# 192 bytes of padding in front of the norm's output: one SBUF offset for both operands of the large products

## The chip, the cores and the metric

The kernel runs on one core of one Trainium2 chip, as one launch. Times are device microseconds; the kernel before takes 1121.89 us (median of 3 runs, 1121.78 to 1123.58). TensorE (PE) multiplies: an instruction LDWEIGHTS puts a 128 x 128 operand into the array (the stationary operand, `lhsT`), and MATMUL streams the other one (the moving operand, `rhs`) past it into a bank of PSUM. VectorE (DVE) and ScalarE (ACT) work on the tiles in SBUF, and SyncE (SP) issues nearly all DMAs. SBUF has 128 partitions; a tile's address is its byte offset in each partition. This text calls the address modulo 2048 the residue of a tile.

## The reference, cut to what matters

One decoder layer with 512 tokens and a width of 1024, in float32:

```python
h = _rms(x, norm1_w) * (1 + sc1) + sh1               # sc1, sh1, g1, ... = silu(c) @ w_ada + b_ada
z, xbc, dt, q, k, v, u, gates = split(h @ w_in)      # 11,280 columns
x = x + g1 * ((g_ssd*y_ssd + g_attn*y_attn + g_pool*y_pool) @ w_out)
h = _rms(x, norm2_w) * (1 + sc2) + sh2
x = x + g2 * (square(relu(h @ w_ff1)) @ w_ff2)       # 4096 wide between the two
```

`y_ssd`, `y_attn` and `y_pool` are a Mamba-2 scan, a dilated window attention and a pooling over windows, each followed by a projection to 1024 columns. Most of the arithmetic is the large products with `w_in`, `w_ssd_out`, `w_attn_out`, `w_pool_out`, `w_out`, `w_ff1` and `w_ff2`.

## The kernel before, in words

Each large product is done three times over, in float32r: both operands are split into a high part and a low part, and `mm3` (lines 284 to 287) sums low x high, high x high and high x low in one PSUM bank. Three MATMULs of 512 columns, one from each of the lines 285, 286 and 287, make a triple; a 512-column strip of a weight with 1024 rows is 8 x 4 = 32 triples.

Weights come from DRAM two row blocks at a time into `raw` (pool `raws`, three buffers), ACT writes their high part `wh`, and DVE their low part `wl` (pool `wsp`, three buffers each, line 267). `wstream` (line 274) does this ahead of the products by a scheduling priority.

Two forms of product exist. In `gemm_feat` (line 289) the weight tile is stationary, 128 of its columns at a time, and the activation streams. In `gemm_tok` (line 301) it is the other way round: 128 tokens of the activation are stationary and the weight streams. There the 128 tokens either lie one after the other or, for two of the three attention groups (`mod=True`), are every fourth token, so that the stationary operand is read with a step of four elements (`toks`, line 298).

Where the tiles lie, in the order in which the pools are opened (lines 102 to 106) and filled. `cpool` begins at 16512 with `cst` (constants, 328 columns, 1312 bytes) and then holds the 16 tiles of the norm's output, 2048 bytes each: `hh`, `hl` (high and low part after the first norm), whose places `gh`, `gl` take over after the second norm. `sm` has small tiles (`vec`, `ones`, statistics), among them no operand of a large product. Then follow `raws`, `wsp` and `gp`; the latter has the 59 blocks of 2048 bytes from which `blk` takes every other activation (`a` after the squared ReLU, `yn`, `pool`, `o`, `mx`) and the resident weights (`wsh`, `wsl` at the start, `wrh`, `wrl` near the second norm).

What reads the norm's output, by the names of the trace (a row says `psacc<-moving,stationary`, and an ending h or l is the high or low part):

- streaming, from `hh`, `hl` and `gh`, `gl`: rows `psacc<-hl,wh` and its like, 416 triples (13 strips), and `psacc<-gl,wh`, 224 triples (7 strips);
- stationary, tokens one after the other: `psacc<-wsl,hh`, 64 triples (the first query and key strips, lines 456 to 482, in an order written out by hand), and 32 of the 224 triples `psacc<-wl,hh` (the first value strip);
- stationary, every fourth token: the other 192 triples `psacc<-wl,hh`, 6 strips;
- streaming 256 columns at a time past resident weights (`ff_rows`, line 1129): `psacc<-gl,wrh`, 64 triples.

Of the kernel before, what the change touches and what calls it, by code (L numbers as in the profile page):

```python
# [10 lines left out]
F32 = mybir.dt.float32  # L11
# [6 lines left out]
P = 128  # L18
# [80 lines left out]
def kernel(ctx: ExitStack, tc: tile.TileContext, a: dict, out: bass.AP, dbg=None):  # L99
    nc = tc.nc  # L100

    cpool = ctx.enter_context(tc.tile_pool(name="cpool", bufs=1))
# [9 lines left out]
    def uid(s):  # L112
        cnt[0] += 1
        return f"{s}_{cnt[0]}"

    class Slots:
# [12 lines left out]
        def free(self, t):  # L129
            self.idle.append(self.used.pop(id(t))[0])  # L130
# [3 lines left out]
    def blk(name, dt=F32):  # L134
        return sb.take(name, dt)
# [5 lines left out]
    def small(shape, name, bufs=1, dt=F32):  # L141
        return sm.tile(shape, dt, tag=name, name=uid(name), bufs=bufs)
# [13 lines left out]


    ncut = COFF["al0"][0]
    cst = cpool.tile([P, ncut], F32, name="cst")

    def C(name):
        at, width = COFF[name]
        return cst[:, at : at + width]
# [7 lines left out]

    ident, tri = C("ident"), C("tri")
    vec = small([P, NVCOLS], "vec")
    crow = [blk("crow") for _ in range(2)]
    xT = [blk(f"xT{k}") for k in range(8)]
    ones = small([P, P], "ones")
# [155 lines left out]
    with tc.manual_schedule(engines={E.DVE, E.Activation, E.PE, E.SP}):  # L332
# [129 lines left out]
        for k in range(8):  # L462
# [19 lines left out]
            for ch, ps in ((Q, qps), (K, kps)):  # L482
# [1 line left out]
                for j in range(4):  # L484
                    mm3(ps[j], th[:, j, :], tl[:, j, :], wh, wl, k == 0, k == 7)
                free(wh, wl)
    nc.sync.dma_start(cst[:, P:], a["const"][:, P:ncut])
    free(R1)
    show("hT", [h.bitcast(F32) for h in hh + hl])
    qkw = small([P, 1], "qkw")  # L490
# [784 lines left out]
```

## Time and profile before

| | before |
|---|---|
| runs, median of 3 | 1121.89 us |
| profiled execution | 1121.93 us, of which the span is 1120.2 us |
| PE busy | 1112.6 us, 99% of the span, 5414 matmuls |
| PE weight load busy | 948.4 us, 85% |
| DVE, ACT busy | 598.4 us (53%), 491.8 us (44%) |
| DMA | 134.45 MB, mean 120 GB/s |
| TensorE clock granted | 1.00 in every stretch |

The span is that of the program's own instructions; 1.7 us of the execution lie around it. Matmuls are pipelined: the record of one with 512 columns is some 390 ns long, while the next one begins some 230 ns after it. So the pace of PE is read from starts, not from durations: first start, last start and count of a group give the time of one step.

### The profile page before, as it was taken

The numbers are of one execution on the slowest core, as the hardware profiler recorded it, in microseconds if no ns is written. First come the engines' busy times: TensorE is split into PE (matmuls) and PEld (weight loads), VectorE is DVE, ScalarE is ACT, GpSimd is POOL, SyncE is SP. The second block draws the span as 40 slices with busy tenths as digits, with TensorE's granted clock in tenths as the row PEclk, the third lists the DMA queues.
The fourth block names the chain that finished last, engine by engine and source line by source line (L and its number), as shares of the span: only waits on it lengthen the run. The fifth ranks groups of instructions, "written<-read, shape, count | busy, mean of one in ns | idle before, by whom it ended". The sixth has DMA issues, their size and how long they took to land.

```text
span 1120.2 us, 14055 instructions
## 1 busy us (share of the span) xinstructions
PE 1112.6 (99%) x5414; PEld 948.4 (85%) x5414; DVE 598.4 (53%) x1210; ACT 491.8 (44%) x937; POOL 0.2 (0%) x4
## 2 busy tenths in 40 slices
PE   8999999999999999999999999999999999999998
PEld 6889998999887888888888888899888888888887
DVE  6973773582567668478833324576454233445241
ACT  5485886543497448425532123353333111344120
POOL 0000000000000000000000000000000000000000
PEclk9999999999999999999999999999999999999999
DMA  9953253334543444322333423350122322222231
GB/s 337 295 190 102 95 164 100 113 104 132 152 140 114 122 152 132 117 86 71 106 110 113 150 95 101 123 191 1 57 94 94 100 105 96 94 95 94 94 132 38
DMA packets 49347, 134.45 MB, mean 120 GB/s; under 512 B 5616, under 2 KB 6384, under 8 KB 49280
## 3 DMA queue, kind: packets, MB, share of 16 engines
q1 hardware_dynamic: 47696, 130.81, 35.5%
q10 hardware_dynamic: 1584, 2.75, 0.8%
q8 instruction: 42, 0.69, 0.3%
q14 instruction: 25, 0.20, 0.1%
HBM read 131.41 MB, written 2.13 MB: 119 GB/s over the span
## 4 chain that ended last, share of the span: by engine, by line
PE 95%; DMA 2%; ACT 2%; DVE 1%; SPq 0%; issue 0%; DVEq 0%; ACTq 0%
PE psacc L285 29%; PE psacc L287 29%; PE psacc L286 29%; PE psS L555 1%; DMA wa<-in_w_ada_dram 1%; PE psy L867 1%; PE pso L671 1%; PE psyo L875 1%; PE pso L669 1%; DVE conv L786 0%; DMA wst<-in_w_in_dram 0%; PE pskT L539 0%; PE psqT L534 0%; PE pspT L652 0%; DMA xT<-in_x_dram 0%; PE psst L827 0%
## 5 line engine op out<-in xcount | busy, mean ns | idle before, releaser
L271 DVE TENSOR_TENSOR wl<-raw,wh 128x1024 fp32r<-128x1024 f32 x161 | 197.1, 1224 | 344.4 <-ACT wh L270 342.6
L270 ACT CAST wh<-raw 128x1024 fp32r<-128x1024 f32 x161 | 168.7, 1049 | 374.5 <-PE psacc L286 323.8
L285 PE MATMUL psacc<-hl,wh 128*128 128x512 f32 x416 | 167.9, 404 | 0.5 <-ACT prev L830 0.4
L287 PE MATMUL psacc<-hh,wl 128*128 128x512 f32 x416 | 163.3, 393 | 0.0
L286 PE MATMUL psacc<-hh,wh 128*128 128x512 f32 x416 | 162.1, 390 | 0.0
L285 PE MATMUL psacc<-wl,hh 128*128 128x512 f32 x224 | 93.4, 419 | 0.0
L287 PEld LDWEIGHTS psacc<-hh,wl 128*128 128x128 f32 x416 | 78.1, 188 | 18.1
L285 PEld LDWEIGHTS psacc<-hl,wh 128*128 128x128 f32 x416 | 78.3, 188 | 17.8 <-issue 1.2
L286 PEld LDWEIGHTS psacc<-hh,wh 128*128 128x128 f32 x416 | 78.2, 188 | 17.8 <-issue 1.4
L286 PE MATMUL psacc<-ah,wh 128*128 128x512 f32 (+1 forms) x242 | 92.2, 381 | 0.0
L285 PE MATMUL psacc<-al,wh 128*128 128x512 f32 (+1 forms) x242 | 92.1, 381 | 0.0
L287 PE MATMUL psacc<-ah,wl 128*128 128x512 f32 (+1 forms) x242 | 92.1, 380 | 0.0
L286 PE MATMUL psacc<-wh,hh 128*128 128x512 f32 x224 | 90.1, 402 | 0.0
L287 PE MATMUL psacc<-wh,hl 128*128 128x512 f32 x224 | 89.7, 401 | 0.0
L285 PE MATMUL psacc<-gl,wh 128*128 128x512 f32 x224 | 88.1, 393 | 0.0
L286 PE MATMUL psacc<-gh,wh 128*128 128x512 f32 x224 | 87.5, 391 | 0.0
L287 PE MATMUL psacc<-gh,wl 128*128 128x512 f32 x224 | 87.3, 390 | 0.0
L286 PEld LDWEIGHTS psacc<-wh,hh 128*128 128x128 f32 x224 | 65.9, 294 | 1.4
L285 PEld LDWEIGHTS psacc<-wl,hh 128*128 128x128 f32 x224 | 65.4, 292 | 1.7
L287 PEld LDWEIGHTS psacc<-wh,hl 128*128 128x128 f32 x224 | 65.5, 293 | 1.5
L235 DVE SCALAR_TENSOR_TENSOR wa<-wa,crow 128x512 f32<-128x512 f32 x64 | 43.4, 688 | 22.0 <-DMA wa<-in_w_ada_dram 22.0
L286 PEld LDWEIGHTS psacc<-ah,wh 128*128 128x128 f32 x242 | 45.5, 188 | 8.8
(342 smaller groups left out, 1908.6 us busy)
## 6 DMA issues: line engine op xcount, KB each, us to landing
raw<-in_w_in_dram SPq DMA_DIRECT2D x80, 512.0 KB, 3.5
raw<-in_w_ff_dram SPq DMA_DIRECT2D x64, 512.0 KB, 3.4
wa<-in_w_ada_dram SPq DMA_DIRECT2D x96, 256.0 KB, 4.5
wst<-in_w_in_dram SPq DMA_DIRECT2D x16, 256.0 KB, 5.4
M<-prow SPq DMA_DIRECT2D x16, 256.0 KB, 3.4
raw<-in_w_ssd_out_dram SPq DMA_DIRECT2D x8, 512.0 KB, 3.5
raw<-in_w_pool_out_dram SPq DMA_DIRECT2D x8, 512.0 KB, 3.5
raw<-in_w_out_dram SPq DMA_DIRECT2D x8, 512.0 KB, 3.4
```

The lines of the kernel that those rows point to most:

```text
L235: V.scalar_tensor_tensor(wa[i], wa[i], 1.0, crow[i], ALU.mult, ALU.mult, accum_out=d[:, i : i + 1])
L270: S.copy(wh, raw)
L271: V.tensor_tensor(wl, raw, wh.bitcast(F32), ALU.subtract)
L285: mm(ps, lhsT=wh, rhs=xl, start=first, stop=False)
L286: mm(ps, lhsT=wh, rhs=xh, start=False, stop=False)
L287: mm(ps, lhsT=wl, rhs=xh, start=False, stop=last)
L555: mm(so[b], lhsT=qT[:, b * P : (b + 1) * P], rhs=kT[:, (b + 1) * P - n : (b + 1) * P], start=True, stop=True)
L669: mm(od, lhsT=vs[kb][:, hs], rhs=pT[b // 2][:, cs : cs + P], start=(b == 0), stop=False, skip_group_check=True)
L671: mm(ov[:, b, :], lhsT=vs[b][:, hs], rhs=pT[0][:, b * P : (b + 1) * P], start=False, stop=(gi == 2 and b == 3), skip_group_check=True)
L867: mm(yp[half * 64 : half * 64 + 64, cs], lhsT=X[c][:, (2 * j + half) * 64 : (2 * j + half + 1) * 64], rhs=Ms[half][:, cs], start=True, sto ...
L875: mm(op[:, cs], lhsT=prev[c][:, j * P : (j + 1) * P], rhs=CT[:, cs], start=True, stop=True)
```

## The change

Two paddings. `cst` becomes 48 columns (192 bytes) wider; its DMA still writes the same columns. And `sm` gets a tile `gap` of 464 columns (1856 bytes) that nothing reads or writes. 192 + 1856 is 2048, so whatever lies behind `gap` moves by 2048 bytes and keeps its residue. Only `vec` and the 16 tiles of the norm's output get another residue. The addresses in the two compiled programs:

| tiles | before: first address, residue | after: first address, residue |
|---|---|---|
| `hh`, `hl`, `gh`, `gl` (16 tiles) | 17824, **1440** | 18016, **1632** |
| `raw` | 65120, 1632 | 67168, 1632 |
| `wh`, `wl` | 77408, 1632 | 79456, 1632 |
| the 59 blocks of `gp` | 101984, 1632 | 104032, 1632 |
| `vec` (150 columns of scalars) | 50592, 1440 | 50784, 1632 |
| `ones` | 51200, 0 | 53248, 0 |

The instructions, their order on each engine and their waits are the same in both programs, but for the numbers in the tiles' names.

```diff
-    cst = cpool.tile([P, ncut], F32, name="cst")
+
+    cst = cpool.tile([P, ncut + 48], F32, name="cst")
...
     vec = small([P, NVCOLS], "vec")
+    small([P, 464], "gap")
     crow = [blk("crow") for _ in range(2)]
...
-    nc.sync.dma_start(cst[:, P:], a["const"][:, P:ncut])
+    nc.sync.dma_start(cst[:, P:ncut], a["const"][:, P:ncut])
```

## Rows read from the trace of the kernel before

**Rows 1.** The page: span, busy time by engine, clock by slices.
```profile
span 1120.2 us, 14055 instructions
PE 1112.6 (99%) x5414; PEld 948.4 (85%) x5414; DVE 598.4 (53%) x1210; ACT 491.8 (44%) x937; POOL 0.2 (0%) x4
...
PEclk9999999999999999999999999999999999999999
```

**Rows 2.** PE's waits: us in total, times, longest.
```profile
PE pssx L404 <- DVE sq L403: 1.7, 1, 1.7
PE pswarm L392 <- DVE ones L352: 1.1, 1, 1.1
PE psacc L285 <- ACT prev L830: 0.4, 1, 0.4
PE psacc L287 <- DVE hl L450: 0.4, 1, 0.4
```

**Rows 3.** Line 285, two stretches: durations min/median/max ns, first and last start.
```profile
L285 PE MATMUL psacc<-al,wh x106: 389/389/390, 866.2 to 937.6; 128*128 128x512 f32 x106
...
L285 PE MATMUL psacc<-gl,wh x95: 394/394/395, 949.9 to 1014.5; 128*128 128x512 f32 x95
```

**Rows 4.** Lines 285, 286, 287 over the span: `h` and `yn` streaming.
```profile
L285 PE MATMUL psacc<-hl,wh x416: 388/394/798, 266.6 to 695.3; 128*128 128x512 f32 x139
...
L285 PE MATMUL psacc<-ynl,wh x64: 389/389/398, 564.5 to 629.5; 128*128 128x512 f32 x64
...
L286 PE MATMUL psacc<-hh,wh x416: 387/388/482, 267.0 to 695.5; 128*128 128x512 f32 x139
...
L286 PE MATMUL psacc<-ynh,wh x64: 387/389/392, 564.8 to 629.7; 128*128 128x512 f32 x64
...
L287 PE MATMUL psacc<-hh,wl x416: 388/392/480, 267.2 to 695.7; 128*128 128x512 f32 x139
...
L287 PE MATMUL psacc<-ynh,wl x64: 389/389/397, 565.0 to 629.9; 128*128 128x512 f32 x64
```

**Rows 5.** Line 285, `h` stationary: start, first value strip, every fourth token.
```profile
L285 PE MATMUL psacc<-wsl,hh x53: 393/394/395, 29.7 to 66.1; 128*128 128x512 f32 x53
...
L285 PE MATMUL psacc<-wl,hh x16: 394/394/399, 181.3 to 191.8; 128*128 128x512 f32 x16
...
L285 PE MATMUL psacc<-wl,hh x16: 398/400/404, 66.8 to 77.5; 128*128 128x512 f32 x16
```

**Rows 6.** Line 286, weight loads over the span.
```profile
L286 PEld LDWEIGHTS psacc<-ah,wh x242: 187/188/193, 854.0 to 1099.9; 128*128 128x128 f32 x121
L286 PE MATMUL psacc<-ah,wh x242: 282/389/398, 854.2 to 1100.0; 128*128 128x512 f32 x111, 128*128 128x256 f32 x10
L286 PEld LDWEIGHTS psacc<-wh,hh x224: 187/309/334, 66.8 to 263.8; 128*128 128x128 f32 x112
...
L286 PEld LDWEIGHTS psacc<-wsh,hh x64: 187/187/190, 20.7 to 66.1; 128*128 128x128 f32 x64
```

**Rows 7.** Line 286, 256 columns, two stretches.
```profile
L286 PE MATMUL psacc<-mxh,wrh x39: 283/283/284, 740.0 to 753.7; 128*128 128x256 f32 x39
...
L286 PE MATMUL psacc<-gh,wrh x27: 279/279/280, 779.4 to 788.6; 128*128 128x256 f32 x27
```

**Rows 8.** DVE's timeline: start us, us; two successive steps of the first products.
```profile
37.91 0.75 DVE L450 SCALAR_TENSOR_TENSOR hl<-u,A,hh 128x512 fp32r<-128x512 f32 x1
...
43.30 0.75 DVE L450 SCALAR_TENSOR_TENSOR hl<-u,A,hh 128x512 fp32r<-128x512 f32 x1
```

**Rows 9.** Busy time by stretch: stretch, length, engines, clock, DMA.
```profile
20.00:60.00 40.00, 39.13 (x165) 30.42 (x165) 39.37 (x110) 19.33 (x32) 0.00 (x0) 1.00 0.95 323
60.00:200.00 140.00, 140.00 (x659) 131.10 (x658) 79.05 (x218) 99.92 (x340) 0.00 (x0) 1.00 0.37 123
...
260.00:560.00 300.00, 299.42 (x1516) 245.95 (x1516) 207.21 (x409) 163.18 (x242) 0.00 (x0) 1.00 0.39 121
```

## The prediction

> **What bounds the kernel now.** I read the page's first lines, then PE's waits, then line 285 stretch by stretch, because the change alters no instruction: all that it can alter is how long instructions take. PE is busy for 1112.6 of 1120.2 us at a granted clock of 1.00, the upper level of 2.4 GHz, in every slice [rows 1], and its waits are 1.7 us at most, four of them together 3.6 us [rows 2]. So a matmul that PE does sooner ends the kernel sooner, as long as the other engines keep up.
>
> What to see next is the pace of the triples, (last start - first start) / (count - 1) [rows 3]. With `a` streaming (residue 1632, like its weights) a triple takes (937.6 - 866.2) / 105 = 680.0 ns. With `g` streaming (residue 1440, weights 1632) it takes (1014.5 - 949.9) / 94 = 687.2 ns. Same shapes, same weight pool, same loop, no wait in either. The starts are known to 0.1 us, so each figure is good to about 1 ns, and the 7 ns are real. The durations say the same and say it of `h` too: the three lines' medians are 394 + 388 + 392 = 1174 ns with `h` and 389 + 389 + 389 = 1167 ns with `yn`, which lies in `gp` and stands in the middle of the `h` products [rows 4]. Among the products of 512 columns that stream past contiguous weights, the norm's output alone is off the even 389, and it alone has another residue. That is the row on which this forecast stands; the trace shows the difference, not its cause.
>
> **The change part by part.**
>
> *Padding itself.* `gap` has no instruction, the DMA into `cst` moves the same columns, `vec` holds scalars. All weights and blocks keep their residue and their distance from each other. I cost this at nothing: no instruction and no transfer is added that could be late.
>
> *Norm's output streaming, 416 + 224 = 640 triples.* The residue becomes that of `a` and `yn`, so each triple should come down from 687 to 680: 640 x 7 = 4.48 us. All of it is on the path, PE being the chain. Bounds: nothing, if the residue is not the cause; 4.6 us with the 7.2 ns of the pace [rows 3].
>
> *Norm's output stationary, tokens one after the other, 64 + 32 triples.* Here the pace is (66.1 - 29.7) / 52 = 700.0 ns at the start and (191.8 - 181.3) / 15 = 700 ns in the value strip [rows 5]. The distance between stationary and moving residue has the other sign than in the case above, and the loss is larger: 20 ns against 680. No row has a stationary operand of `h` with equal residues, so bounds: nothing and 96 x 20 = 1.92 us. I take the upper end, because the weight load itself is as long as that of `a` (187 and 188 ns [rows 6]), the matmul is of the same shape, and nothing else tells the two cases apart. Of this the first row block's eight triples (0.16 us) are lost again: PE then waits 0.4 us for DVE's `hl` [rows 2], and will wait the longer. That leaves 1.76 us.
>
> What hides behind PE at the start is DVE, busy for 39.37 of 40 us [rows 9]: one step of its loop takes 43.30 - 37.91 = 5.39 us [rows 8]. PE's step is 8 triples, 5.60 us now and 5.44 us after. DVE stays 0.05 us faster, so PE remains the bound, narrowly. If that cover is gone, 7 x 0.16 = 1.1 us of the gain go.
>
> *Norm's output stationary, every fourth token, 192 triples.* The pace is (77.5 - 66.8) / 15 = 713 ns [rows 5], and the load has a median of 309 ns instead of 188 [rows 6]. That load goes over all 2048 bytes of a tile, not over 512, so an equal first address need not mean what it means elsewhere. Nothing in the trace shows such a load with equal residues. Bounds: above, the pace of `a`, 192 x 33 = 6.3 us gained; below nothing, a loss, if the 309 ns no longer run beside the stream: (3 x 309 - 713) x 192 = 41 us lost. The nearest row is the contiguous one, same tiles and same weights [rows 5], which gains 20 per triple; the step's own 13 ns above it stays. Because the walk is another one I take half, 10 ns: 192 x 10 = 1.92 us, and keep 0 and 3.84 us as the inner bounds.
>
> A page of the Trainium skill has the step's part of this: "SBUF — State Buffer", in its specifications, says that each crossing to a new line of 16 bytes pays a penalty, and every fourth float32 is in a line of its own. By that the 309 ns are the step's price, the residue cannot take them away, and this term would be nearer to nothing; the sum is then 1116.1.
>
> *Second norm, 256 columns past resident weights, 64 triples.* Here the sign turns. `mx` with equal residues takes (753.7 - 740.0) / 38 = 360.5 ns a triple, `g` with unequal ones (788.6 - 779.4) / 26 = 353.8 ns [rows 7]. The two loops differ in how many banks they fill in turn, so this may not be the residue at all. Bounds: nothing, and 64 x 6.7 = 0.43 us lost; I take the loss.
>
> *Sum.* 4.48 + 1.76 + 1.92 - 0.43 = 7.73 us. The profiled execution took 1121.93 us (span 1120.2), which is the median of the runs to 0.04 us, so 1121.9 - 7.7 = **1114.2 us**. With the term of every fourth token at 0 and 3.84 the forecast's own range is 1116.1 to 1112.3.
>
> **The rivals.**
>
> *The residue is not the cause; nothing changes: 1121.9 us.* The norm's output also differs from `gp` by its place, below the weights instead of above them, and that stays. For it: the sign turns at 256 columns [rows 7], which one simple rule does not explain. Against it: 59 blocks spread over 120 KB all stream at 389 [rows 4, 6], so place as such does not show, while one residue differs. The Trainium skill speaks for this rival: "TensorE: Matmul & The Clock Gate", in its step-by-step part, gives PE two independent SBUF read ports, so that loading the next weights takes nothing from the running matmul. By that rule no address could matter and the time would stay at 1121.9; the 7 and 20 ns of [rows 3, 5] speak against it, since these triples differ in no instruction.
>
> *The loads with a step get worse: slower.* With an equal start the load of 2048 bytes and the stream of 2048 bytes go over the same offsets from their first element on, and the stream may stall until the load is through. The place is the 192 triples between 67 and 264 us. Wholly serial they cost 41 us, for 1121.9 + 41 - 5.8 = 1157 us; the kernel is slower from 5.81 / 192 = 30 ns per triple on, 743 instead of 713. For it: this load is already the longest and its pace the worst [rows 5, 6], and equal residues are slower at 256 columns. Against it: in `a` equal starts are the best case there is [rows 3]. A mild form, 0 to 20 ns lost per triple, ends between 1116.1 and 1120.
>
> *The feed becomes the bound.* If DVE's step at the start grows past 5.44 us, 1.1 us go, for 1115.3 us. Later ACT is busy for 99.92 of 140 us in the worst stretch [rows 9], too little to hold PE at a pace that is 1 to 3% faster.
>
> *Loads with a step come all the way to 680 ns:* 6.3 instead of 1.92, for 1109.8 us.
>
> **How the numbers follow.** Forecast with its own range 0.66; nothing changes 0.10; mild loss in the stepped loads 0.08; the feed 0.06; all the way 0.05; clearly slower 0.05. A measurement of this kernel can tell about 0.2%, 2.2 us, from no change. Faster than 1119.7: 0.66 + 0.06 + 0.05 and most of the 0.08, 0.84. Within: 0.11. Slower: 0.05. The range goes from 1110.5, below which lies most of the case "all the way", to 1119.0, above which lie "nothing changes", the slower case and the edge of the mild one, together about 0.2.
>
> **What would show it.** The medians of lines 285, 286, 287 with `h` and `g` should read 389, 389, 389, and `g`'s pace in its second run 680. `wsl,hh` should go from 700 to 680, and `wl,hh` with the step from 713 to about 703. `gh,wrh` should read 283 instead of 279. PE's busy share stays at 99% and its waits where they are. The prediction is wrong if `h` still reads 394, 388, 392, or if the stepped triples pass 743.

## The result, and the profile after

The changed kernel takes 1115.98 us (median of 5, 1115.43 to 1119.5), the kernel before beside it 1122.32 (5 runs); the ratio is 0.9948, 95% interval 0.9931 to 0.9965. That is 6.3 us less, where 7.7 were forecast. In the profiled executions the span falls from 1120.2 to 1114.3 us, by 5.9.

The page of the kernel after, against [rows 1]: PE is busy for 7.4 us less, and it idles for 1.5 us more, so that the span is 5.9 us shorter.

```profile
span 1114.3 us, 14055 instructions
...
PE 1105.2 (99%) x5414; PEld 946.8 (85%) x5414; DVE 598.0 (54%) x1210; ACT 491.5 (44%) x937; POOL 0.2 (0%) x4
```

The lines 285 to 287 are 287 to 289 now. The norm's output streaming, durations min/median/max over the span, as in [rows 4]: 394, 388, 392 have become three times 389, as `yn` had all along.

```profile
L287 PE MATMUL psacc<-hl,wh x416: 387/389/793, 263.6 to 690.7; 128*128 128x512 f32 x139
...
L288 PE MATMUL psacc<-hh,wh x416: 387/389/480, 263.9 to 690.9; 128*128 128x512 f32 x139
...
L289 PE MATMUL psacc<-hh,wl x416: 388/389/473, 264.2 to 691.1; 128*128 128x512 f32 x139
```

The paces, as in [rows 3, 5]: `g` streaming takes (1008.9 - 944.9) / 94 = 680.9 ns a triple instead of 687.2, `a` beside it 680.2 as before. Stationary, the start takes (64.8 - 28.7) / 53 = 681.1 instead of 700.0, and the first value strip (189.3 - 178.4) / 16 = 681 instead of 700.

```profile
L287 PE MATMUL psacc<-al,wh x107: 389/389/389, 860.6 to 932.7; 128*128 128x512 f32 x107
...
L287 PE MATMUL psacc<-gl,wh x95: 389/389/389, 944.9 to 1008.9; 128*128 128x512 f32 x95
...
L287 PE MATMUL psacc<-wsl,hh x54: 389/389/395, 28.7 to 64.8; 128*128 128x512 f32 x54
...
L287 PE MATMUL psacc<-wl,hh x17: 389/389/400, 178.4 to 189.3; 128*128 128x512 f32 x17
```

At 256 columns [rows 7] `g` has become as slow as `mx`: 283 ns, and (784.3 - 774.9) / 26 = 361.5 ns a triple instead of 353.8.

```profile
L288 PE MATMUL psacc<-mxh,wrh x40: 282/283/283, 735.0 to 749.0; 128*128 128x256 f32 x40
...
L288 PE MATMUL psacc<-gh,wrh x27: 280/283/283, 774.9 to 784.3; 128*128 128x256 f32 x27
```

And PE's waits, against [rows 2]: one has grown from 0.4 to 1.1 us, two of 0.4 and 0.2 us are new, and the one for `sq` at the start is 1.9 us instead of 1.7. That is the 1.5 us.

```profile
PE psacc L287 <- ACT prev L832: 1.1, 1, 1.1
...
PE psrr L213 <- DVE diag L212: 0.4, 1, 0.4
PE pskT L541 <- DVE k L510: 0.2, 1, 0.2
```

Where the 5.9 us come from. PE's order being the same in both traces, each uninterrupted stretch of one kind can be taken from its first start to the first start behind it, waits included, and compared with its counterpart:

| stretches on PE | forecast, us | measured, us |
|---|---|---|
| `h` streaming | -2.91 (416 x 7) | -1.21 |
| `g` streaming | -1.57 (224 x 7) | -1.51 |
| `h` stationary, the start | -1.12 (64 x 20 less 0.16) | -1.04 |
| `h` stationary, first value strip | -0.64 (32 x 20) | -0.53 |
| `h` stationary, every fourth token | -1.92 (192 x 10) | -1.45 |
| `g`, 256 columns | +0.43 | +0.39 |
| `a`, `yn`, `pool`, `pd` streaming | 0 | -0.42 |

### The profile page after: what moved, and what is told of

The parts are those of the page before. It is cut to its first block, busy times and chain, and to the rows that moved or that the text cites. A ratio compares the mean times of both kernels' runs of the same rounds, so it can differ in the third digit from the quotient of the medians.

```text
span 1114.3 us, 14055 instructions
## 1 busy us (share of the span) xinstructions
PE 1105.2 (99%) x5414; PEld 946.8 (85%) x5414; DVE 598.0 (54%) x1210; ACT 491.5 (44%) x937; POOL 0.2 (0%) x4
## 4 chain that ended last, share of the span: by engine, by line
PE 92%; DMA 3%; ACT 3%; DVE 2%; issue 0%; SPq 0%; DVEq 0%; ACTq 0%
PE psacc L287 28%; PE psacc L288 28%; PE psacc L289 28%; DMA wa<-in_w_ada_dram 1%; PE psS L557 1%; PE psy L869 1%; DMA M<-prow 1%; PE pso L673 1%; PE psyo L877 1%; PE pso L671 1%; ACT wh L272 1%; DVE conv L788 0%; DMA wst<-in_w_in_dram 0%; PE pskT L541 0%; PE pspT L654 0%
## 5 line engine op out<-in xcount | busy, mean ns | idle before, releaser
L287 PEld LDWEIGHTS psacc<-al,wh 128*128 128x128 f32 x242 | 45.5, 188 | 8.8
```

What stands on the lines that cost most here:

```text
L287: mm(ps, lhsT=wh, rhs=xl, start=first, stop=False)
```

## The experiments

The theory (D): what counts is the distance between the residues of the two operands, not where each lies. Its rivals: the residue 1440 itself is a bad place to start (R); the period is 2048 bytes, as the change's wording has it; the padding or the higher addresses helped in another way.

**1. Equal residues the other way round.** `gap` stays, `cst` keeps its old width: all operands at 1440.

```diff
-    cst = cpool.tile([P, ncut + 48], F32, name="cst")
+    cst = cpool.tile([P, ncut], F32, name="cst")
```

> The other way to equal residues: cst keeps its width, so the norm's output stays at 1440, and gap alone moves all weights and blocks from 1632 to 1440. Theory D (what counts is the distance between the residues of the stationary and the moving operand): like the changed kernel, 1116 us, and all streaming triples at 680 ns. Theory R (1440 itself is a bad place to start): the norm's output keeps 687 and 700 ns, and a, yn, pool, o and mx, some 480 triples, get 687 as well: 1122 + 3.4 = 1125 us.

Measured: 1115.32 us, ratio to before 0.9951 (0.9933 to 0.9968; every ratio here is to the kernel before, run beside it, with its 95% interval). `a` and `g`, now at 1440 with their weights, read 389 ns; `g`'s pace is (1007.4 - 944.1) / 93 = 680.6. R falls.

```profile
L287 PE MATMUL psacc<-al,wh x107: 389/389/389, 861.8 to 933.9; 128*128 128x512 f32 x107
...
L287 PE MATMUL psacc<-gl,wh x94: 389/389/389, 944.1 to 1007.4; 128*128 128x512 f32 x94
```

**2. Only the first padding.** The norm's output goes to 1632, the rest to 1824.

```diff
-    small([P, 464], "gap")
```

> Only the first padding: the norm's output goes to 1632 as in the changed kernel, and without gap everything behind it goes to 1824, so the distance stays 192 bytes. Theory D: like before, 1122 us, with h and g streaming at 687 ns a triple and stationary at 700. Theory R: 1632 is the good residue, so 1116 us or a little more, if 1824 is bad for the rest.

Measured: 1122.0 us, ratio 1.0002 (0.9992 to 1.0012), `g` at 394 ns and (1014.9 - 949.7) / 95 = 686.3 a triple. The residue of the changed kernel without the equal distance brings nothing.

```profile
L286 PE MATMUL psacc<-gl,wh x96: 394/394/394, 949.7 to 1014.9; 128*128 128x512 f32 x96
```

**3 and 4. Eight distances in one trace.** Each row block `k` of the norm's output gets its own distance above the weights, and a letter in its name; `gap` shrinks by the sum of the paddings.

```diff
+LET = "ABCDEFGH"
+PADS = [0, 32, 32, 32, 32, 32, 32, 32]      # bytes; the far one: [256, 64, 64, 64, 64, 512, 512, 320]
...
+            if PADS[k]:
+                cpool.tile([P, PADS[k] // 4], F32, name=f"pad{k}", tag=f"pad{k}")
+            hh.append(cpool.tile([P, T], F32R, name=f"h{LET[k]}h", tag=f"hh{k}"))
+            hl.append(cpool.tile([P, T], F32R, name=f"h{LET[k]}l", tag=f"hl{k}"))
```

> Each of the eight row blocks of the norm's output gets its own distance above the weights' residue, 0, 32, 64, 96, 128, 160, 192, 224 bytes (letters A to H in the tiles' names), so that one trace has eight paces. Theory D: A reads 389, 389, 389 ns and 680 a triple; the others differ by distance. If only stationary minus moving counts, with its sign, G (192) streaming loses 20 ns as the stationary case of before did, and G stationary loses 7. Theory R: only the absolute residue counts, so the eight may differ, but the two roles of one tile then lose alike.

> The same with distances of 256, 320, 384, 448, 512, 1024, 1536 and 1856 bytes (A to H). 1856 is the distance of the kernel before, so H must show 394, 388, 392 and 687 ns streaming, 700 stationary. Theory D with a period of 512 bytes (the four 512-byte column slices of a weight tile read alike before): E, F and G read 680 like a distance of 0, streaming and stationary, and B (320) reads like H. With a period of 2048 E, F and G differ from 680.

One execution of each: 1126.28 us (near) and 1122.16 us (far). One of the three lines with `h` streaming, near (A is 0, then steps of 32 bytes): only A has the even 389 (C, D, F and H, not shown, have 394 or 395).

```profile
L291 PE MATMUL psacc<-hAh,wl x52: 388/389/398, 266.3 to 678.5; 128*128 128x512 f32 x52
...
L291 PE MATMUL psacc<-hBh,wl x52: 392/396/397, 269.0 to 681.2; 128*128 128x512 f32 x52
...
L291 PE MATMUL psacc<-hEh,wl x52: 390/394/404, 283.9 to 689.6; 128*128 128x512 f32 x52
...
L291 PE MATMUL psacc<-hGh,wl x52: 393/394/399, 292.8 to 695.2; 128*128 128x512 f32 x52
```

The same in the far run (D is 448, E 512, F 1024, G 1536, H 1856 bytes): the multiples of 512 read 389, and H reads the 392 of the kernel before.

```profile
L290 PE MATMUL psacc<-hDh,wl x52: 392/394/400, 276.8 to 684.2; 128*128 128x512 f32 x52
...
L290 PE MATMUL psacc<-hEh,wl x52: 389/389/398, 283.0 to 687.0; 128*128 128x512 f32 x52
...
L290 PE MATMUL psacc<-hFh,wl x52: 388/389/397, 285.7 to 689.7; 128*128 128x512 f32 x52
...
L290 PE MATMUL psacc<-hGh,wl x52: 389/389/397, 291.8 to 692.4; 128*128 128x512 f32 x52
...
L290 PE MATMUL psacc<-hHh,wl x52: 392/392/477, 294.6 to 695.2; 128*128 128x512 f32 x52
```

The paces go further than these durations. For each matmul, the time from its start to the next start was sorted by the distance (address of the next stationary operand minus address of the streaming one, modulo 512); the medians of the three lines added up are the pace of a triple, in ns. (All weights have one residue, so these traces do not tell whether the next stationary operand counts or the one in the array.)

| stationary minus moving, modulo 512 | 0 | 64 | 128 | 192 | 256 | 320 | 384 | 448 | other multiples of 32 |
|---|---|---|---|---|---|---|---|---|---|
| `h`, `g` streaming | 681 | 699 | 696 | 687 | 688 | 697 to 700 | 695 | 687 | 698 to 701 |
| `h` stationary, neighbouring tokens | 680 | 702 | 696 | 687 | 682 | 700 | 695 | 687 | 700 to 702 |

Both roles of the norm's output follow nearly one curve; at 256 it is the least even, 685 with `h` and 692 with `g`. The 7 ns and the 20 ns of the kernel before are the same thing at +192 and at -192, which is 320. The period is 512 bytes here, shorter than the change's 2048: the streaming column 0 holds the distances 0, 512, 1024 and 1536.

**5 and 6. All tiles 64 and all tiles 512 bytes off.**

```diff
-    cst = cpool.tile([P, ncut + 48], F32, name="cst")
+    cst = cpool.tile([P, ncut + 64], F32, name="cst")       # 512 bytes: ncut + 176
...
-    small([P, 464], "gap")
+    small([P, 448], "gap")                                  # 512 bytes: 336
```

> All 16 tiles of the norm's output 64 bytes above the weights' residue, everything else as in the changed kernel. If the paces by distance of the two many-distance runs add up to the time: streaming goes from 680 back to 687 (stationary minus moving is 448 modulo 512), 640 x 7 = 4.5 us; stationary with neighbouring tokens from 680 to 702, 96 x 21 = 2.0 us; every fourth token from 709 to 716, 192 x 7 = 1.3 us; 256 columns 6 ns less a triple, 0.4 us back. Sum 1116 + 7.4 = 1123 us, no better than before the change, although the padding is as large. If it is the padding as such, or the higher addresses, that helped: 1116 us.

Measured: 1122.05 us, ratio to before 0.9998 (0.9989 to 1.0008). `g` takes (1014.6 - 950.0) / 94 = 687.2 ns a triple, and the start (65.8 - 30.1) / 51 = 700. All of the padding is there, and all of the gain gone.

```profile
L287 PE MATMUL psacc<-gl,wh x95: 393/395/395, 950.0 to 1014.6; 128*128 128x512 f32 x95
...
L287 PE MATMUL psacc<-wsl,hh x52: 393/395/395, 30.1 to 65.8; 128*128 128x512 f32 x52
```

> All 16 tiles 512 bytes above the weights' residue, everything else as in the changed kernel. If the period is 512 bytes: 1116 us, all medians at 389 ns streaming and for neighbouring tokens. If the residue modulo 2048 has to be equal: 687 to 700 ns a triple and 1121 us or more.

Measured: 1116.19 us, ratio 0.9944 (0.9927 to 0.996), and (1009.4 - 946.1) / 93 = 680.6 ns with `g`. The period of 512 bytes holds in the time too.

```profile
L287 PE MATMUL psacc<-gl,wh x94: 388/389/390, 946.1 to 1009.4; 128*128 128x512 f32 x94
```

**7. The distance of before with its sign turned.** `cst` 96 columns wider, `gap` 416: all 16 tiles 192 bytes above the weights.

> All 16 tiles 192 bytes above the weights' residue: the distance of the kernel before with its sign turned. If stationary minus moving counts with its sign, streaming now gets what the stationary case of before had, 698 ns a triple, and the stationary case gets 687: 640 x 18 + 96 x 7 = 12.2 us more, some 1 us more for the stepped loads, 1.2 us less at 256 columns, together 1116 + 12 = 1128 us. If only the size of the distance counts, the time is that of before, 1122 us.

Measured: 1127.82 us, ratio to before 1.0049 (1.0034 to 1.0064). `g` streaming takes (1020.4 - 955.3) / 93 = 700.0 ns, the start (65.4 - 29.0) / 53 = 686.8: the two roles have changed places. At 256 columns it is the best of all: the record is 276 ns long where equal residues have 283 and the kernel before had 279, and from start to start a triple takes 341 ns instead of 360 and 354. There equal residues are not the optimum.

```profile
L287 PE MATMUL psacc<-gl,wh x94: 394/394/394, 955.3 to 1020.4; 128*128 128x512 f32 x94
...
L287 PE MATMUL psacc<-wsl,hh x54: 388/388/388, 29.0 to 65.4; 128*128 128x512 f32 x54
...
L288 PE MATMUL psacc<-gh,wrh x64: 276/276/283, 768.4 to 792.8; 128*128 128x256 f32 x64
```

(The second row shows why the pace is read from starts: its median of 388 ns is below the 389 of equal residues, but its pace is 686.8 ns and theirs 681.)

**8. The grown wait.** In the changed kernel, ACT's copy of the scan's first state gets a higher priority; it moves ahead of one evacuation of `z`. The edit gave DVE's writes of `diag` the higher priority too, but the order of the instructions on PE, ACT and DVE is otherwise that of the changed kernel.

```diff
-            V.tensor_scalar(dg, ident, r[:, b : b + 1], None, ALU.mult)
+            with tc.high_priority(offset=SOON):
+                V.tensor_scalar(dg, ident, r[:, b : b + 1], None, ALU.mult)
...
                 if d == 0:
-                    S.copy(pv, sp)
+                    with tc.high_priority(offset=SOON):
+                        S.copy(pv, sp)
```

> The changed kernel with one instruction moved: ACT copies the scan's first state one 0.6 us evacuation earlier, which frees the PSUM bank on which PE now waits 1.1 us. If that wait is where part of the streaming gain was given back, it falls to about 0.5 us and the span by 0.6 us, to 1113.7; if ACT as a whole is late there, the wait comes back at the next matmul and the span stays at 1114.3.

One execution: 1115.25 us, span 1113.5 instead of 1114.3. The time alone would not show a gain, since the changed kernel's own executions have spans from 1113.6 to 1114.3 us and one of 1117.7; the trace does. First the changed kernel's PE in time order, start and duration in us, then this kernel's: the wait falls from 1.11 to 0.23 us, where 0.5 was expected. From start to start this place takes 0.88 us less, and all the rest together 0.03 us more.

```profile
347.41 0.39 PE L289 MATMUL psacc<-hh,wl 128*128 128x512 f32 x1
348.91 0.50 PE L287 MATMUL psacc<-hl,wh 128*128 128x512 f32 x1 [1.11 <-ACT prev L832]
```

```profile
347.51 0.39 PE L290 MATMUL psacc<-hh,wl 128*128 128x512 f32 x1
348.13 0.50 PE L288 MATMUL psacc<-hl,wh 128*128 128x512 f32 x1 [0.23 <-ACT prev L834]
```

**9. Another distance for the stepped loads.** The weight buffers get 512 bytes more, and the six strips with every fourth token use them from byte 352 on, which makes the distance 160 modulo 512.

```diff
-        wh = wsp.tile(shape, F32R, tag="wh", name=uid("wh"))
-        wl = wsp.tile(shape, F32R, tag="wl", name=uid("wl"))
+        n = shape[1] * shape[2]
+        wh, wl = (wsp.tile([P, n + 128], F32R, tag=t, name=uid(t))[:, off : off + n].rearrange("p (a t) -> p a t", a=2) for t in ("wh", "wl"))
...
-        for k, wh, wl in wstream(w, nk, ch, 0, ahead):
+        for k, wh, wl in wstream(w, nk, ch, 0, ahead, 88 if mod else 0):
```

> The changed kernel, but for the six strips whose stationary tokens are every fourth one the weights are written 352 bytes into longer buffers, so that the norm's output lies 160 bytes above them modulo 512; all other distances stay 0. In the many-distance run this distance gave the stepped triples 701 to 702 ns instead of 706 to 710. If that holds for all 192 triples: 0.9 to 1.3 us less, 1114.9 us, and medians of 393 to 395 ns. If it was chance among 24 triples: 1116 us.

Measured: 1115.31 us, ratio to before 0.9941 (0.9926 to 0.9956), span 1113.8. The stepped triples take 702 ns from start to start (mean without interruptions over 260 ns) instead of 706 in the changed kernel and 714 before, so 24 triples had not misled. The durations show less of it: their medians are 397 here and 398 to 400 there, where 393 to 395 was expected. 192 x 4 ns are 0.8 us, below the 0.9 to 1.3 us expected; 0.5 arrive in the span, while the wait on `diag` grows from 0.4 to 0.6. Against the changed kernel the time alone does not tell it from no change.

**10. Both together.**

> The distance of 160 bytes for the stepped strips and the scan's first copy moved forward, in one kernel. If the two small gains are independent, the span falls by their sum, 0.5 + 0.8 = 1.3 us, to 1113.0, and the time to some 1114.7 us; if the earlier strips' gain only makes PE wait longer for the same copy, the span stays near 1113.5.

Measured: 1114.78 us, ratio to before 0.9934 (0.9922 to 0.9947), the lowest median of all, though the intervals overlap. The profiled execution has a span of 1113.4 us where 1113.0 was expected if the two gains added up; the median span of the five executions is 1113.0, against 1114.2 of the changed kernel. In the profiled trace the wait on `prev` is gone, the one on DVE's `diag` is 1.2 us and the one for `sq` at the start 2.3. That the earlier arrival of PE causes the longer wait on `diag` is not shown: it differs from trace to trace also where nothing was moved (0 in experiment 1, 0.9 us in experiment 6).

```profile
PE pssx L406 <- DVE sq L405: 2.3, 1, 2.3
PE psrr L213 <- DVE diag L212: 1.2, 1, 1.2
```

## Why the prediction was right, and where it was not

- *The cause.* Right, and now shown: with equal distance at another residue the gain is there (1), with the new residue and the old distance it is not (2), and the distance alone moves the time from 1116 to 1128 us (5 to 7). The rival "nothing changes" falls; by the rule of the Trainium skill on two independent read ports, "TensorE: Matmul & The Clock Gate", step-by-step part, no distance could matter, and here a triple takes 680 to 702 ns by it. What inside PE or SBUF makes the distance count, no row shows, and no run here tried to.
- *Norm's output streaming, 640 x 7 = 4.48 us, "all of it on the path".* This is the term that was mis-sized: 2.72 us came. `g` gave what was forecast, 1.51 of 1.57. `h` gave 1.21 of 2.91, for two reasons. First, 1.0 us became waits: PE came sooner to the bank that `prev` frees and to `diag`, and ACT and DVE did not come sooner by as much (+0.7 and +0.3 us from start to start). So "its waits where they are" was wrong. Experiment 8 shows it for the first: moving the copy alone takes 0.88 us off that wait. I had asked of every engine's load whether it could hold PE, and 99.92 of 140 us said no; but a chain that PE waits for once is late whatever the load. How much goes this way differs from trace to trace: with the same paces it is 0.3 us in experiment 1 and 1.5 us in experiment 6, and `h` gains 1.94 and 0.72 us there, while every other forecast row of the table agrees within 0.07 us. The waits on `prev` and `diag` read 0.9 and nothing there, and 1.0 and 0.9 us. Second, 152 of the 416 triples stand in 19 blocks of 24 matmuls behind transposes or small products. After such an interruption the first matmul takes over 300 ns and the next ten 229 to 230 ns on average before and 228 to 231 after; only then do they settle, at 229 and at 227. With the two waits set aside these blocks gain 0 to 0.05 us each (one loses 0.01), where eight triples at 7 ns are 0.056. That is another half microsecond. One such block, from start to start in ns, before and after:

```
before: 321 235 231 232 226 229 232 226 229 231 226 229 232 226 229 232 226 229 231 226 229 232 226
after:  313 229 233 236 224 231 236 228 233 231 226 227 227 226 227 227 226 227 227 226 227 227 226
```

- *Norm's output stationary, neighbouring tokens.* Right: 1.57 of 1.76 us. The start stayed PE's, as the 0.05 us of cover allowed. The loss that was put at 0.16 us and at DVE's `hl` is 0.10 us and stands at ACT's `hh`; the wait for `hl` is 0.4 us in both traces.
- *Every fourth token.* The choice of half, for which no row spoke, was near by luck: 1.45 of 1.92 us, at 706 ns a triple. The Trainium skill's rule on lines of 16 bytes ("SBUF — State Buffer", specifications), by which this term goes towards nothing, agrees with the trace as far as the load goes, which still takes 310 ns (309 in [rows 6]). The term did not go to nothing: the pace came down by 8 ns, though not to 680. The rival that such loads get worse, for a slower kernel, did not come.
- *256 columns.* Right in sign and size, and the doubt whether it is the residue at all is settled: `g` takes 360 ns a triple at a distance of 0, 354 at 192, 341 at 320, in one and the same loop (the kernel after, before, and 7).
- *Not in the sum:* streams that were at equal distance before, `yn`, `pool`, `pd` and `a`, gained 0.42 us. The traces show where: in the first ten matmuls behind a block of `h` or `g`. With `yn` and `pool` these take 231.6 ns on average in the kernel before and all later ones 226.7; in the changed kernel all take 226.7. In experiments 2 and 5, whose distance is not 0, the ten take 231.6 to 231.7 ns again, in 7 228.7, and in 1 and 6 226.6 to 226.7. So a stream paid up to 50 ns wherever the distance had changed just before it. Starts behind `h`, in ns, before and after:

```
yn before: 234 231 233 236 224 231 236 228 233 230 227 227
yn after:  227 226 227 227 226 227 227 226 227 227 226 227
```

- *The number.* The sum came within 1.8 us of the time, partly by luck: 1.76 us too much in the streaming term stands against 0.42 us that were not in the sum.

## What to carry to other kernels

When PE is busy for 99% of the span and its matmuls of one shape run at different paces, compare the addresses of the two operands: here the padding cost no time of its own, and a kernel with another distance for each of eight tiles gave eight paces in a single trace. What it was worth here is 0.5% of the time. Read the pace from starts, not from durations. And ask of a faster PE not only whether the other engines have time, but which single instruction it will now reach before its releaser.

## What the runs showed of the hardware that was not expected

- The pace of float32r triples of 512 columns follows stationary minus moving address, in these runs with a period of 512 bytes and with the sign counting: 680 to 681 ns at 0, 682 to 688 at 256, 687 at 192 and 448, 695 to 702 at the other multiples of 32. At two distances the absolute place was changed as well, and made no difference (1, 2).
- With 256 columns the order is another one: 360 ns at 0, 341 at 320.
- A stationary operand read with a step of 16 bytes runs at 701 to 718 ns, and its best distance among those tried was 160, not 0.
- After an interruption, or a change of distance, some ten matmuls run at 228 to 232 ns on average before the stream settles at 227, where its distance is 0.
